# The broadcast gate rows of a hybrid mLSTM / DeltaNet block, issued from GpSimd's DMA queue instead of SyncE's

## The chip, the cores and the metric

The kernel runs on one core of a Trainium2 chip. A core has five engines that run side by side, each with its own instruction stream executed in order: TensorE (PE in the profile; its weight loads are PEld), VectorE (DVE), ScalarE (ACT), GpSimd (POOL) and SyncE (SP), which here does nothing but issue transfers. Transfers are carried by 16 DMA engines; SP, ACT and POOL can each issue them, and each has a queue of its own (q1 is SP's, q10 is ACT's, q0 is POOL's in the profile's table). An engine that issues a transfer waits, in its own stream, until the transfer's target may be overwritten, and the engine that uses the data waits for a semaphore that the landed transfer raises. The metric is device time in microseconds (us) of one launch; lower is better.

## The reference

One decoder layer on 512 tokens of width 2048, all in float32: an RMSNorm, one wide projection, two causal token mixers (8 mLSTM heads and 16 gated DeltaNet heads), an output projection per branch, a gated sum and a final RMSNorm. What matters here is where one number per token and head enters a token-by-token matrix:

```python
# mLSTM: one running gate sum b and one running maximum per head and token
dmat = bcum[..., :, None] - bcum[..., None, :] + ic[..., None, :]
m_t = jnp.maximum(inter_log, dmax_c)
inter_w = jnp.exp(inter_log - m_t)
intra_w = jnp.exp(dm_c - m_t[..., None]) * sc_c
# DeltaNet: one decay sum gam per head and token
rel = gam[..., :, None] - gam[..., None, :]
decay_mat = jnp.where(incl, jnp.exp(jnp.where(incl, rel, 0.0)), 0.0)
q_dec = qc * jnp.exp(gam)[..., None]
```

In each of these the number belongs to the query token `t`. The kernel keeps the query tokens along the free axis of a tile, so that number has to be present in every one of the 128 partitions.

## The kernel before, in words

Matrix products are done in pairs of float32r parts: each weight chunk is loaded (`wr`), rounded to a high part on ACT (`wh`, line 135) and its remainder is formed on DVE (`wl`, line 138), and TensorE multiplies three products per pair. Four chunks may be loaded ahead and four may be split ahead (`NRAW`, `NSPL`).

The stages follow each other: the RMSNorm and the first query and key projections; four kinds of wide projections with a seven-product scheme (to about 1060 us of the span); the mixers with the remaining projections (about 1060 to 1900 us); the output projections and the final norm.

In the gate stage near the start, the per-head rows are computed once with the heads in partitions and stored to a small DRAM tensor `rows_d` of 32 rows by 512 tokens: rows 0 to 7 hold the mLSTM exponents, 8 to 15 the mLSTM inter-chunk weights, 16 to 31 the DeltaNet decay sums (lines 459, 469, 470).

The mixers run as eight DeltaNet units of two heads each (`dn_unit`), `p` = 0 to 7. A unit projects keys, values and queries of its two heads (and, for `p` = 3 to 6, also queries and keys of one mLSTM head, 4 to 7); the mLSTM heads 0 to 3 were projected early and run beside the first units (`ml_first`). Around these projections, small generators (`dn_front_k`, `dn_front_q`, `dn_back`, `dn_chain`, `ml_head`) put out the mixers' own instructions; `tick()` advances them, and `yield n` lets n groups of matmuls go by. The order on TensorE is the order of the program text. On the other four engines a planner that simulates the program's time line orders the instructions: by readiness, by priority (`urgent` raises it) and by the fixed neighbours given with `behind`. Each engine then runs its list strictly in order.

The steps that use the gate rows:

- DeltaNet: `dn_front_k` asks for the rows of its two heads with `row_bcast` (line 760; tile `gb`). GpSimd makes from each a masked copy `dm` (line 823); ScalarE exponentiates `dm` (line 832) and then `gb` in place (line 833); GpSimd copies the last column of each chunk (`ge`, line 834) and much later multiplies the queries with `gb` (line 920).
- mLSTM: `ml_head` asks for one row with `row_bcast` (tile `nrb`) and for one with line 1090 (tile `iwb`). GpSimd makes the masked copy `wm` from `nrb` (line 1093), ScalarE exponentiates it (line 1098); GpSimd takes the last columns of `iwb` (`de`, line 1109) and multiplies the queries with it (line 1111).

`gb` and `nrb` share three buffers (tag `rb`); the last reader of a `gb` is line 920 and the only reader of an `nrb` is line 1093, both on GpSimd. `iwb` shares three buffers (tag `tg`) with the transposed queries `qn` and, in other stages, with other tiles. Every load copies one row of 512 float32 (2 KB) into each of 128 partitions: 256 KB.

Besides these, GpSimd has in a unit the small power functions of the norms (lines 873, 1036, 1157), products with broadcast columns (lines 872, 896, 1037, 1160) and copies of the inverted blocks (lines 937, 940). It issues transfers only after the mixers: the accumulating stores of the output (`y_d`, lines 1339 and 1440).

Of the kernel before, what the change touches and what calls it, by code (L numbers as in the profile page):

```python
# [15 lines left out]
P = 128  # L16
# [39 lines left out]
def hybrid_body(  # L56
# [16 lines left out]
    nc = tc.nc  # L73
    ctx.enter_context(tc.manual_schedule(engines={mybir.EngineType.PE}))
    V, A, G, T = nc.vector, nc.scalar, nc.gpsimd, nc.tensor
# [5 lines left out]
    rows_d = dr.tile([32, S], F32, tag="rows", name="rows_d")  # L81
# [666 lines left out]
    for i in range(NYP):  # L748
        t = wkb.tile([P, S + 3], F32, tag=f"yp{i}", name=f"yp{i}", bufs=1)
# [7 lines left out]

    def row_bcast(r, name):
        t = wk.tile([P, NC, P], F32, tag="rb", name=name, bufs=3)
        nc.sync.dma_start(t.rearrange("p c t -> p (c t)"), rows_d[r, :].partition_broadcast(P))  # L760
        return t

    def bc(col, n):
# [53 lines left out]

    def dn_front_k(hs, kq, u):
        rbs = [row_bcast(16 + h, "gb") for h in hs]
        yield 4  # L820
        for j in range(2):
# [221 lines left out]
    def dn_unit(p, mh):  # L1043
# [13 lines left out]
        if mh is not None:  # L1057
            ps = proj_cm(mh, kind="m")
            mkq = wkb.tile([P, 2, S], F32, tag="mkq", name="mkq", bufs=1)
            with urgent():  # L1060
                A.mul(mkq[:, 1, :], ps[0], float(P) ** -0.5)
            with urgent():
                A.copy(mkq[:, 0, :], ps[1])
            start(ml_head(mh, mkq), 1, "B")
# [18 lines left out]
    def ml_head(h, kq):  # L1083
        kT, qT = kq[:, 0, :], kq[:, 1, :]
        kw = wkb.tile([P, NC, P], F32, tag="mkw", name="kw", bufs=1)
        with behind("V"):
            turn(kT, kw)
        rb = row_bcast(h, "nrb")
        iwb = wp.tile([P, NC, P], F32, tag="tg", name="iwb", bufs=3)
        nc.sync.dma_start(iwb.rearrange("p c t -> p (c t)"), rows_d[8 + h, :].partition_broadcast(P))  # L1090
        yield 4
        w = wkb.tile([P, NC, P], F32, tag="mw", name="wm", bufs=1)
        G.affine_select(out=w, in_=rb, pattern=[[0, NC], [1, P]], channel_multiplier=-1, base=0,
# [74 lines left out]
    def ml_first(h):  # L1168

        kq = wkb.tile([P, 2, S], F32, tag="mkq", name="mkq", bufs=1)  # L1170
        for i in range(2):
            nc.sync.dma_start(kq[:, 1 - i, :], qk_d[2 * QKFIRST * i + h])
        yield 4
        yield from ml_head(h, kq)
# [481 lines left out]
```

## Time and profile before

| | us |
|---|---|
| median of 3 runs | 2229.91 (2222.15 to 2234.51) |
| the profiled execution, its own time | 2228.3 |
| its span, first to last instruction | 2226.5 |
| PE busy | 2157.8 (97% of the span) |
| DVE busy | 1650.0 (74%) |
| ACT busy | 1022.2 (46%) |
| POOL busy | 265.2 (12%) |

The span is what the trace covers; the time of a run is a little longer. Busy time is the sum of an engine's instructions. Where an engine is idle, the profile names the instruction or transfer that ended the idle time. In a row of the time line stand the start, the duration, the engine, the source line, the operation, the target and the source, how many instructions are merged, and in brackets the idle time before with its releaser; a "q" behind the engine marks its sequencer, which issues transfers. A row of transfers "us to landing" counts from the issue until the semaphore is raised.

### The profile page before, as it was taken

How to read it: one execution, taken by the hardware profiler on the slowest of the kernel's cores; microseconds unless marked ns; L12 is line 12 of the kernel's file. 1: busy time of each engine (PE TensorE's matmuls, PEld its weight loads, DVE VectorE, ACT ScalarE, POOL GpSimd, SP SyncE). 2: the span in 40 equal slices, each digit the busy share in tenths (PEclk: the TensorE clock that was granted, in tenths of full speed). 3: DMA queues.
4: the chain of work that ended last, by engine and by line, in shares of the span. 5: the costliest groups of instructions: out<-in, count | busy, mean ns of one | idle time of the engine just before them, and what ended most of it. 6: DMA issues, size and time to landing. Idle time of an engine off the chain costs nothing. (4 is left out here: it accounts for less than half of the span.)

```text
span 2226.5 us, 31649 instructions
## 1 busy us (share of the span) xinstructions
PE 2157.8 (97%) x10592; PEld 1770.6 (80%) x10592; DVE 1650.0 (74%) x2883; ACT 1022.2 (46%) x1986; POOL 265.2 (12%) x356
## 2 busy tenths in 40 slices
PE   6999999999999999999999999999999999989997
PEld 5877878888788788888888788888787887867775
DVE  5787788788778777877597786757575777567776
ACT  5444444445444444444545544444444454334344
POOL 0320000000000000000222412212122211110101
PEclk9999999999999999999999999999999999999999
DMA  5456666667667766776776767767666668695896
GB/s 156 124 176 197 196 202 198 209 200 234 192 211 232 236 197 215 231 241 190 198 201 165 172 161 174 165 160 172 161 145 162 152 157 230 176 268 184 247 323 220
DMA packets 534821, 435.81 MB, mean 196 GB/s; under 512 B 241921, under 2 KB 393698, under 8 KB 534530
## 3 DMA queue, kind: packets, MB, share of 16 engines
q1 hardware_dynamic: 425058, 357.68, 56.3%
q10 hardware_dynamic: 105568, 68.77, 9.7%
q0 software_dynamic: 4032, 7.34, 2.2%
q8 instruction: 83, 1.36, 0.2%
q14 instruction: 80, 0.66, 0.1%
HBM read 342.37 MB, written 95.49 MB: 197 GB/s over the span
## 5 line engine op out<-in xcount | busy, mean ns | idle before, releaser
L135 ACT CAST wh<-wr 128x512 fp32r<-128x512 f32 (+1 forms) x538 | 379.2, 706 | 416.3 <-PE pj L262 229.3
L138 DVE TENSOR_TENSOR wl<-wr,wh 128x512 fp32r<-128x512 f32 (+1 forms) x538 | 440.9, 822 | 152.9 <-ACT wh L135 142.7
L261 PE MATMUL pj<-uh,wh 128*128 128x512 f32 x1024 | 428.6, 419 | 0.0
L263 PE MATMUL pj<-uh,wl 128*128 128x512 f32 x1024 | 402.6, 393 | 0.0
L262 PE MATMUL pj<-ul,wh 128*128 128x512 f32 x1024 | 402.1, 393 | 0.0
L576 PE MATMUL ps<-wl,uh 128*128 128x512 f32 x704 | 277.7, 394 | 6.7 <-DVE wl L138 6.5
L575 PE MATMUL ps<-wh,uh 128*128 128x512 f32 x704 | 276.1, 392 | 6.3 <-DVE X L617 6.0
L577 PE MATMUL ps<-wh,ul 128*128 128x512 f32 x704 | 274.9, 391 | 0.0
L135 ACT CAST wh<-ts 128x512 fp32r<-128x512 f32 x224 | 138.2, 617 | 258.2 <-DVE ts L535 199.7
L135 ACT CAST wh<-t 128x1024 fp32r<-128x1024 f32 x112 | 117.8, 1052 | 250.0 <-PE ps L577 129.2
L263 PEld LDWEIGHTS pj<-uh,wl 128*128 128x128 f32 x1024 | 193.4, 189 | 42.6
L576 PE MATMUL ps<-wl,suh 128*128 128x512 f32 x576 | 224.3, 389 | 1.7 <-DVE wl L138 1.7
L575 PE MATMUL ps<-wh,suh 128*128 128x512 f32 x576 | 224.4, 390 | 0.6 <-ACT wh L135 0.3
L577 PE MATMUL ps<-wh,sul 128*128 128x512 f32 x576 | 224.1, 389 | 0.0
L261 PEld LDWEIGHTS pj<-uh,wh 128*128 128x128 f32 x1024 | 194.3, 190 | 35.2
L262 PEld LDWEIGHTS pj<-ul,wh 128*128 128x128 f32 x1024 | 194.3, 190 | 32.9
L138 DVE TENSOR_TENSOR wl<-ts,wh 128x512 fp32r<-128x512 f32 x224 | 153.7, 690 | 38.5 <-ACT wh L135 38.5
L138 DVE TENSOR_TENSOR wl<-t,wh 128x1024 fp32r<-128x1024 f32 x112 | 137.7, 1229 | 47.5 <-ACT wh L135 46.6
L576 PEld LDWEIGHTS ps<-wl,uh 128*128 128x128 f32 x704 | 132.3, 188 | 43.6 <-DVE wl L138 17.3
L575 PEld LDWEIGHTS ps<-wh,uh 128*128 128x128 f32 x704 | 132.3, 188 | 40.1 <-DVE X L617 12.4
L577 PEld LDWEIGHTS ps<-wh,ul 128*128 128x128 f32 x704 | 132.5, 188 | 26.6
L535 DVE TENSOR_TENSOR ts<-wr 128x512 f32<-128x512 f32 x112 | 77.3, 690 | 102.8 <-DMA wr<-t_d 77.0
(302 smaller groups left out, 3475.6 us busy)
## 6 DMA issues: line engine op xcount, KB each, us to landing
wr<-in_w_in_dram SPq DMA_DIRECT2D x704, 256.0 KB, 3.7
wr<-in_w_out_dram SPq DMA_DIRECT2D x138, 256.0 KB, 5.1
t_d<-ts ACTq DMA_DIRECT2D x96, 256.0 KB, 4.0
wr<-t_d SPq DMA_DIRECT2D x96, 256.0 KB, 4.0
wr<-in_w_in_dram SPq DMA_DIRECT2D x64, 128.0 KB, 3.4
xt<-in_x_dram SPq DMA_DIRECT2D x8, 512.0 KB, 7.3
tg_d<-X ACTq DMA_DIRECT2D x16, 256.0 KB, 6.1
tg_d<-to ACTq DMA_DIRECT2D x16, 256.0 KB, 5.7
```

Of the source, the lines that this page charges most:

```text
L135: newest["A"] = A.copy(hi, src).ins
L138: newest["V"] = V.tensor_tensor(out=lo, in0=src, in1=hi.bitcast(F32), op=ALU.subtract).ins
L261: T.matmul(ps[j], hi[:, k, wsl], uh[:, kt, :], start=(kt == 0), stop=False)
L262: T.matmul(ps[j], hi[:, k, wsl], ul[:, kt, :], start=False, stop=False)
L263: T.matmul(ps[j], lo[:, k, wsl], uh[:, kt, :], start=False, stop=(kt == KT - 1))
L535: V.tensor_tensor(out=ts[:, 0, :], in0=r[:, 0, :], in1=r[:, 2, :], op=ALU.subtract)
L575: T.matmul(ps[t], ah, hi, start=(g == "A" and i == 0), stop=False, skip_group_check=True)
L576: T.matmul(ps[t], ah, lo, start=False, stop=False, skip_group_check=True)
L577: T.matmul(ps[t], al, hi, start=False, stop=(i == KH - 1), skip_group_check=True)
```

## The change

Two calls name another engine; nothing else is edited. `G` is `nc.gpsimd`. With 16 calls of `row_bcast` for `gb`, 8 for `nrb` and 8 loads of `iwb`, 32 transfers of 256 KB move from SP's queue to GpSimd's, and they enter GpSimd's in-order list beside its computing instructions.

```diff
     def row_bcast(r, name):
         t = wk.tile([P, NC, P], F32, tag="rb", name=name, bufs=3)
-        nc.sync.dma_start(t.rearrange("p c t -> p (c t)"), rows_d[r, :].partition_broadcast(P))
+        G.dma_start(t.rearrange("p c t -> p (c t)"), rows_d[r, :].partition_broadcast(P))
         return t
...
         rb = row_bcast(h, "nrb")
         iwb = wp.tile([P, NC, P], F32, tag="tg", name="iwb", bufs=3)
-        nc.sync.dma_start(iwb.rearrange("p c t -> p (c t)"), rows_d[8 + h, :].partition_broadcast(P))
+        G.dma_start(iwb.rearrange("p c t -> p (c t)"), rows_d[8 + h, :].partition_broadcast(P))
         yield 4
```

## The prediction

> **What bounds the kernel now.** I read the page's busy times first, then the stretches, then what TensorE waits for in the stretch that the change touches.
>
> ```profile
> span 2226.5 us, 31649 instructions
> ...
> PE 2157.8 (97%) x10592; PEld 1770.6 (80%) x10592; DVE 1650.0 (74%) x2883; ACT 1022.2 (46%) x1986; POOL 265.2 (12%) x356
> ```
>
> ```profile
> 1100.00:1900.00 800.00, 786.48 (x4539) 655.39 (x4539) 574.11 (x1435) 386.55 (x1010) 193.53 (x257) 0.99 0.70 169
> 1900.00:2226.50 326.50, 299.24 (x1334) 240.47 (x1332) 230.30 (x338) 135.42 (x229) 27.58 (x32) 0.98 0.78 238
> ```
>
> The columns after the length are the busy times of PE, PEld, DVE, ACT and POOL. In the mixers TensorE is idle for only 800.00 − 786.48 = 13.5 us. That is all that any change of a queue can win there; POOL in the same stretch is idle for 800.00 − 193.53 = 606 us. The last stretch has another 326.5 − 299.2 = 27.3 us, but none of the moved loads lies in it. What TensorE waits for in the mixers, from the waits between 1061 and 1910 us (us in total, times, longest):
>
> ```profile
> PE p L974 <- ACT s L970: 4.3, 3, 1.9
> PE pw L1006 <- DVE tb L976: 4.2, 3, 1.9
> ```
>
> These two, 8.5 us together, are its largest waits there. Neither names a gate row. So the question is whether the moved loads, now late only for GpSimd, get late enough for ACT, DVE and at last TensorE.
>
> **What the moved loads cost on SP now.** The two source lines, then who waits for their data, with the landing times (first line 760, then 1090):
>
> ```profile
> L760 SPq DMA_DIRECT2D gb<-rows_d x16: 332/360/552, 1075.3 to 1780.9; - x16
> L760 SPq DMA_DIRECT2D nrb<-rows_d x8: 339/487/1367, 1072.1 to 1674.8; - x8
> DMA to landing us min/median/max: 3.7/4.4/6.0
> L1090 SPq DMA_DIRECT2D iwb<-rows_d x8: 338/465/1082, 1061.0 to 1666.0; - x8
> DMA to landing us min/median/max: 3.6/4.6/4.7
> ```
>
> ```profile
> POOL de L1109 <- DMA iwb<-rows_d: 20.2, 5, 6.4
> POOL dm L823 <- DMA gb<-rows_d: 15.8, 8, 3.7
> POOL wm L1093 <- DMA nrb<-rows_d: 12.0, 5, 3.6
> ```
>
> SP gets rid of 16 × 0.360 + 8 × 0.487 + 8 × 0.465 = 13.4 us of issuing, spread over 700 us. TensorE's two waits above are not for a weight chunk, so this is worth 0 on its path. Only POOL waits for the rows' data, 48 us in all, of its 606 idle.
>
> **What POOL gets.** No load without accumulation is issued from POOL in this trace, so its cost is bounded by the nearest rows, the accumulating stores of line 1339, and by SP's loads of the same bytes:
>
> ```profile
> L1339 POOL DMA_DIRECT2D y_d<-tgy x8: 860/1006/1470, 1893.9 to 1962.3; - x8
> DMA to landing us min/median/max: 4.4/6.9/9.1
> ```
>
> Issue: between SP's 0.36 and 1.47 us; I take the median 1.01, the same engine and form. 32 × 1.01 = 32 us, so POOL's busy time goes from 265 to about 297 us, beside 606 idle: 0 on the path by itself. Landing: 4.4 (as on SP) to 9.1 us. These stores also read and add, a load does not, so the load should be nearer to the store's median from below; I take 6.9, which is 2.5 us later than now. A gate row would then be 1.0 + 2.5 = 3.5 us late. Is there cover? One steady unit, on POOL and SP:
>
> ```profile
> 1666.02 0.47 SPq L1090 DMA_DIRECT2D iwb<-rows_d  x1
> 1670.88 0.33 POOL L1109 COPY de<-iwb 128x4 f32<-128x4 f32 x1 [6.40 <-DMA iwb<-rows_d]
> 1671.17 1.27 POOL L920 TENSOR_TENSOR kq<-kq,gb 128x512 f32<-128x512 f32 x1
> 1672.47 0.34 SPq L760 DMA_DIRECT2D gb<-rows_d  x1
> 1677.05 0.63 POOL L823 TENSOR_SCALAR_AFFINE_SELECT dm<-gb 128x512 f32<-128x512 f32 x1 [2.71 <-DMA gb<-rows_d]
> 1680.37 0.64 POOL L1093 TENSOR_SCALAR_AFFINE_SELECT wm<-nrb 128x512 f32<-128x512 f32 x1 [2.68 <-DMA nrb<-rows_d]
> 1696.92 0.19 POOL L834 COPY ge<-gb 128x4 f32<-128x4 f32 x1 [15.92 <-ACT gb L833]
> ```
>
> The load of `gb` leaves SP at 1672.47, 0.03 us after line 920 has ended (1671.17 + 1.27 = 1672.44): what frees the buffer is POOL's own instruction. Put into POOL's list behind it, this load adds no new wait, only its issue. Three loads (`iwb`, `gb`, `nrb`) follow in a row here; chained on POOL they make its list late by up to 3 × 1.0 + 2 × 2.5 = 8 us at `wm` (the `iwb` wait and one shared wait for the rows). Behind `wm` POOL has nothing until `ge`, after 15.92 us of idling for ACT. So 8 of 15.9 us are used, and the price is 0. If that cover were gone, `ge` and then DVE's line 847 would be late by the rest.
>
> The other reader is ACT's exponent of `dm`. Its smallest distance over the eight units is in the second one:
>
> ```profile
> 1158.10 0.63 POOL L823 TENSOR_SCALAR_AFFINE_SELECT dm<-gb 128x512 f32<-128x512 f32 x1 [2.65 <-DVE tmp L889]
> 1172.39 1.26 ACT L832 ACTIVATE dm<-dm,ngam 128x128 f32<-128x128 f32 x4
> ```
>
> 1172.39 − 1158.73 = 13.7 us, against 3.5 to 8: covered too. One place has no distance, the first mLSTM head:
>
> ```profile
> 1072.32 0.96 POOL L753 MEMSET tb<- 128x1024 f32 x1 [41.67 <-DMA wr<-in_w_in_dram]
> 1075.31 0.64 POOL L1093 TENSOR_SCALAR_AFFINE_SELECT wm<-nrb 128x512 f32<-128x512 f32 x1 [0.84 <-DMA nrb<-rows_d]
> 1076.33 1.28 ACT L1098 ACTIVATE wm<-wm,acol 128x128 f32<-128x128 f32 x4
> ```
>
> ACT takes `wm` 0.38 us after it is there. With the load 3.5 us later (up to 6 if it also queues behind the 0.96 us memset and its neighbours), ACT stands still that long, and weight splits queue behind it. Their cover is the stock of split chunks:
>
> ```profile
> ACT wh L135 <- PE pj L262: 202.8, 135, 4.0
> ```
>
> ACT waits 135 times for TensorE to give a split buffer back, that is, all four are usually full; one chunk here is 12 matmuls, about 12 × 0.39 = 4.7 us by the page's 393 ns rows (L262, L263), so three chunks ahead are some 14 us. Price 0; the 41.67 us of idling also hide the issue of the first two `iwb` loads.
>
> ```profile
> L262 PE MATMUL pj<-ul,wh 128*128 128x512 f32 x1024 | 402.1, 393 | 0.0
> ```
>
> **A possible gain, and a loss.** TensorE's wait for `s` (line 970) has a cause that the moved loads lie beside:
>
> ```profile
> 1673.73 3.53 ACTq L806 DMA_DIRECT2D hm_d<-to  x2
> 1682.27 0.59 ACT L970 ACTIVATE s<-p 64x512 f32<-64x512 f32 x1 [4.21 <-DMA hm_d<-to]
> ```
>
> ACT needs 3.53 us to issue two stores, while SP issues its own loads, the `nrb` among them. If issuing from two engines at once is what slows them, taking 0.49 us out of those 3.53 gives back a seventh of the 8.5 us: −1.2 us; bounds 0 and −8.5. [...]
>
> The loss is where POOL's list leads to DVE:
>
> ```profile
> 1234.96 1.01 POOL L1036 TENSOR_TENSOR rsd<-ssq,mhalf 128x4 f32<-128x4 f32 x1 [18.49 <-DVE ssq L1034]
> 1240.15 0.19 POOL L1109 COPY de<-iwb 128x4 f32<-128x4 f32 x1 [4.18 <-DMA iwb<-rows_d]
> 1241.37 0.69 DVE L1040 TENSOR_TENSOR gz<-po,gz 128x512 f32<-128x512 f32 x1 [3.85 <-POOL gz L1037]
> ```
>
> Here `de` stands in front of the product `gz`, POOL waits 4.18 us for `iwb`, and DVE with it 3.85 us, without any wait of TensorE in the list above for it. The moved load makes this 3.5 us longer; the stock of chunks should cover 7.4 us of 14. I put in +2 us, with bounds 0 and 5 × 3.5 = 17.5 us (every one of the five `iwb` waits passed on whole).
>
> **The sum**, against the profiled execution's own 2228.3 us: 0 (SP) + 0 (POOL's 32 us) − 1.2 + 2 = 2229.1. The median of the runs is 1.6 us above that execution, so 2230.7: 2231 us.
>
> **Rivals.**
> 1. *ACT's queue is relieved fully*: TensorE's 8.5 us go. For it: 3.53 us for two issues is long, and SP is issuing then. Against it: only one of several SP loads leaves that window. 2229.9 − 8.5 = 2221 us.
> 2. *POOL's order passes the lateness on* (the other side): `iwb`'s load and its landing stand in POOL's list ahead of `gz` and the copies for the inverted blocks; DVE stops in order at line 1040. Price 17.5 us, 2247 us. It decides from the point where the wait, 3.85 now, passes the stock of about 14 us, or where TensorE's next small product needs DVE at once. Against it: today's 3.85 us cost TensorE nothing.
> 3. *DVE starves POOL's issuing*: the longest row is 1.47 us to issue and 9.1 to land. If all five `iwb` loads are as late, 5 × (1.47 + 9.1 − 4.6) = 30 us, 2260 us. Against it: the median row is 1.01, in a stretch where DVE is as busy (230.30 of 326.5 us, 71%) as in the mixers (574.11 of 800, 72%). [...]
> 4. *The planner redraws the other lists*: with the loads gone from SP and new entries on POOL, its simulated time line shifts, and near ties on ACT and DVE can fall the other way, in the mixers or behind them. Nothing in the profile says which way; at most the 13.5 us of idle time come back (2216 us), and as much may be lost (2243 us). This is also the way in which the change might not do what it says: a load that the planner puts far down POOL's list comes late whatever its queue costs.
>
> **How the numbers follow.** Half a percent is 11.1 us, about what a measurement of this kernel can tell from no change: 2218.8 to 2241.1. Chances: forecast 0.60 (0.02 of it beyond the lower bound by the scatter of runs, which spans 12 us, 0.03 beyond the upper); rival 1 0.14 (0.05 beyond); rival 2 0.13 (0.11 slower); rival 3 0.03 (slower); rival 4 0.10 (0.06 faster, 0.04 slower). Faster 0.02 + 0.05 + 0.06 = 0.13; slower 0.03 + 0.11 + 0.03 + 0.04 = 0.21; within 0.66. The range 2217 to 2247 us takes in rivals 1 and 2 and leaves out rival 3 and the far side of rival 4.
>
> **What the changed profile would show.** POOL's busy time near 297 us with 32 issues of about 1.0 us on lines 760 and 1090; q0's bytes up by the 32 loads and q1's down; landing of `gb` and `iwb` at 5 to 7 us; POOL's waits for the rows at 60 to 130 us instead of 48 (48 + 32 × 2.5 = 128); PE's idle time between 1100 and 1900 us within some 5 us of 13.5. It would be wrong if DVE's wait at line 1040, or the one of ACT for `wm`, turns up before an idle TensorE (rival 2), if the issues take over 1.5 us (rival 3), if the 3.53 us on ACT's queue shrink together with the waits at lines 974 and 1006 (rival 1), or if TensorE's idle time moves in places without a gate row (rival 4).

## The result, and the profile after

The changed kernel takes 2216.52 us (median, 2214.27 to 2221.79) beside 2229.91 us of the kernel before; the ratio is 0.995 with a 95% interval of 0.9937 to 0.9963. Measured once more beside the last experiments it took 2222.13 us against 2230.99: 0.9961, 0.9949 to 0.9973. So it is faster by some 0.4 to 0.5%. The prediction said 2231 us, range 2217 to 2247. The first measurement lies 0.5 us under that range and just beyond half a percent, the side that had got a chance of 0.13; the second lies inside the range and, by its ratio, within half a percent, which had got 0.66. Both are faster by more than their intervals leave open, where no gain had been forecast.

The profiled execution has an own time of 2217.53 us. Its page begins:

```profile
span 2215.8 us, 31667 instructions
...
PE 2156.6 (97%) x10592; PEld 1770.1 (80%) x10592; DVE 1655.4 (75%) x2883; ACT 1022.3 (46%) x1986; POOL 279.5 (13%) x388
...
q1 hardware_dynamic: 420450, 349.29, 55.3%
q10 hardware_dynamic: 105568, 68.77, 9.8%
q0 software_dynamic: 6592, 15.73, 3.7%
```

All 32 loads are on q0 (the columns are packets, MB and the share of 16 engines). POOL's busy time is up by 279.5 − 265.2 = 14.3 us, where 32 were expected. The issue and landing rows of the two moved lines (first line 760, then line 1090) say why, and POOL's waits for the rows, from 1061 to 1910 us, went down and not up:

```profile
L760 POOL DMA_DIRECT2D gb<-rows_d x16: 536/565/620, 1075.1 to 1769.0; - x16
L760 POOL DMA_DIRECT2D nrb<-rows_d x8: 536/559/571, 1074.4 to 1661.6; - x8
...
DMA to landing us min/median/max: 3.7/4.3/7.7
...
L1090 POOL DMA_DIRECT2D iwb<-rows_d x8: 557/615/775, 1062.1 to 1653.1; - x8
...
DMA to landing us min/median/max: 4.1/4.8/7.8
```

```profile
POOL wm L1093 <- DMA nrb<-rows_d: 12.6, 4, 4.0
...
POOL dm L823 <- DMA gb<-rows_d: 6.1, 6, 2.7
```

An issue costs 0.56 to 0.62 us where 1.01 was taken (16 × 0.565 + 8 × 0.559 + 8 × 0.615 = 18.4 us), and the rows land after 4.3 and 4.8 us, practically as from SP (4.4 and 4.6), where 6.9 was taken. A wait of POOL for `iwb` is not in the list any more.

The time was won in the mixers. The same two stretches, and TensorE's waits between 1061 and 1910 us, all of them:

```profile
1100.00:1900.00 800.00, 793.56 (x4609) 662.07 (x4608) 586.68 (x1450) 391.21 (x1017) 205.20 (x283) 1.00 0.71 173
1900.00:2215.80 315.80, 291.48 (x1268) 234.96 (x1266) 222.74 (x325) 131.51 (x222) 27.27 (x32) 0.97 0.78 238
```

```profile
PE pw L1006 <- DVE tb L976: 4.0, 4, 1.9
PE py L1315 <- ACT yp L770: 2.1, 2, 1.8
PE p L974 <- ACT s L970: 0.3, 1, 0.3
```

TensorE's idle time there is 6.4 us instead of 13.5, and the wait of line 974 went from 4.3 to 0.3 us. TensorE runs the same 10592 matmuls in the same order in both kernels, so the start of each can be compared with the start of the same one before. Up to matmul 4500 (1052 us) the two are 0.6 us apart; at matmul 8750 (1807 us before) the changed kernel is 11.9 us ahead; at matmul 10500, near the end, 8.8 us. So 12.5 us were won in the mixers and some of it was given back after them. Of the 12.5, the idle time explains 7.1. The rest is the granted clock: a window laid on two places of the kernel before (PEclk is the third column from the end) shows 0.50 right behind TensorE's stalls; a matmul of 128x512 takes 0.63 us there where it takes 0.39 before and after, and its next one starts 0.43 us later instead of 0.23.

```profile
1456.80:1460.20 3.40, 3.40 (x19) 2.90 (x18) 2.40 (x4) 2.65 (x5) 0.00 (x0) 0.50 1.01 230
1460.20:1463.60 3.40, 3.40 (x10) 2.63 (x10) 3.37 (x7) 2.14 (x9) 0.00 (x0) 0.50 0.47 101
1576.30:1579.70 3.40, 3.40 (x11) 2.72 (x10) 3.40 (x6) 2.61 (x12) 0.00 (x0) 0.50 0.29 77
```

Three stretches of 3.4 us, 10.2 us in all, at a clock of 0.50 are an estimated 5.1 us lost, and they count as busy (PE 3.40 of 3.40 us in each row). The first follows a stop of 1.91 us of TensorE at line 974 that began at 1454.5, the last a stop of 1.39 us at line 974 (1568.2) and one of 1.91 us at line 1006 (1573.7). The changed kernel's profiled execution has none up to matmul 8750. 7.1 + 5.1 = 12.2 of 12.5 us. What was given back after that goes with the clock, too: up to matmul 10500 the changed kernel has three slow stretches (the first below, behind a stop of 1.77 us at line 1315; then 3.4 us at 1945.6 and 6.8 at 1986.6), the kernel before has one (3.4 us at 1999.5). TensorE is busy for 11.65 us of the three and 3.4 us of the one, so the clock of 0.50 costs the changed kernel by the same estimate some 4 us more there, and 3.1 us were given back.

```profile
1839.80:1843.20 3.40, 3.40 (x9) 2.63 (x10) 3.40 (x9) 2.85 (x6) 0.00 (x0) 0.50 1.20 311
```

### The profile page after: what moved, and what is told of

Same layout as the page of the kernel before. It is cut to its first block, busy times and chain, and to the rows that moved or that the text cites. A ratio compares the mean times of both kernels' runs of the same rounds, so it can differ in the third digit from the quotient of the medians.

```text
span 2215.8 us, 31667 instructions
## 1 busy us (share of the span) xinstructions
PE 2156.6 (97%) x10592; PEld 1770.1 (80%) x10592; DVE 1655.4 (75%) x2883; ACT 1022.3 (46%) x1986; POOL 279.5 (13%) x388
## 4 chain that ended last, share of the span: by engine, by line
PE 71%; DMA 12%; DVE 9%; issue 4%; ACT 2%; SPq 2%; POOL 1%; ACTq 0%; DVEq 0%; POOLq 0%
PE ps L576 10%; PE ps L577 10%; PE ps L575 10%; PE pj L261 9%; PE pj L263 9%; PE pj L262 9%; DVE wl L138 4%; DMA wr<-t_d 4%; DMA wr<-in_w_in_dram 2%; PE py L1315 2%; PE py L1316 2%; PE py L1317 2%; ACT wh L135 1%; SPq L505 1%; DVE X L617 1%
## 5 line engine op out<-in xcount | busy, mean ns | idle before, releaser
L135 ACT CAST wh<-t 128x1024 fp32r<-128x1024 f32 x112 | 117.8, 1052 | 248.6 <-PE ps L577 133.1
```

What stands on the lines that cost most here:

```text
L135: newest["A"] = A.copy(hi, src).ins
```

## What holds ScalarE

The stops at line 974 come from ScalarE's `s` (line 970), and that from ScalarE's stores at line 806. The rows of that line say who waited for these stores, before and after:

```profile
L806 ACTq DMA_DIRECT2D hm_d<-to x64: 309/310/517, 1132.1 to 1796.2; - x64
L806 ACTq DMA_DIRECT2D h_d<-to x64: 309/358/2046, 1244.5 to 1962.1; - x64
...
  ACT wh L135: 15.5, 4
  ACT s L970: 14.0, 3
```

```profile
L806 ACTq DMA_DIRECT2D hm_d<-to x64: 309/310/1210, 1132.5 to 1784.3; - x64
L806 ACTq DMA_DIRECT2D h_d<-to x64: 309/443/2421, 1242.8 to 1951.8; - x64
...
  ACT wh L135: 8.2, 3
  ACT tb L963: 6.3, 2
```

A store of `hm_d` takes 0.31 us to issue, never over 0.52 before. The "3.53 us for two stores" of the prediction is a row in which the time line merged two issues and the wait between them. What lies between can be read from the semaphore that each transfer raises, which the trace numbers. In this program all transfers of SP and ACT raise one of the same eight (100 to 105, 107, 108), given out in turn over both engines (250 or 251 transfers on each in the kernel before); POOL's raise eight others (111 to 118). An issue on a number waits, in its engine's stream, until the previous transfer on that number has landed, whichever engine issued it: for the three held stores below the trace gives that semaphore as what the issue waits for, and on the five numbers of which the trace of the kernel before has every landing, none of 1248 issues starts earlier than 0.016 us behind the previous landing. The kernel before, in the unit that the prediction quoted (worked out from the trace: issue, engine, line, target, semaphore, landing):

```
1672.47 SP  L760 gb    108  lands 1676.93
1674.76 SP  L760 nrb   103  lands 1680.31
1675.41 SP  L1115 v    104  lands 1681.78
1676.95 ACT L806 hm_d  108  (0.02 us after gb)
1680.33 ACT L806 hm_d  103  (0.02 us after nrb)
1681.80 ACT L806 hm_d  104  (0.02 us after v)
```

Three stores in a row were held by three loads of SP, two of them gate rows. ScalarE stood still, `s` started at 1682.27, and TensorE's line 974 at 1682.91. The second wait of TensorE has the same origin. The next rows are DVE and PE of the kernel before, right behind:

```profile
1684.26 0.75 DVE L773 SCALAR_TENSOR_TENSOR kq<-yp,convc,kq 128x512 f32<-128x512 f32 x1 [5.48 <-ACT kq L771]
...
1688.17 0.68 DVE L976 COPY tb<-p 64x512 f32<-64x512 f32 x1
...
1688.91 0.49 PE L1006 MATMUL pw<-vt,tb 128*128 128x128 f32 x2 [1.90 <-DVE tb L976]
```

VectorE had stood 5.48 us waiting for a ScalarE that was held, had to do its queued work first, and came late with `tb`: both waits of TensorE hang on held stores.

Counted over the mixers (1061 to 1910 us; issues that start within 0.15 us of the landing of the previous transfer on their semaphore, and the time that they stood for it), ScalarE was stopped 44 times for 45.8 us before and 29 times for 22.2 us after. Of the 45.8, 9.9 us are `hm_d` behind `nrb`, 9.3 behind `gb`, 5.0 behind `iwb`, and 1.5 are `h_d` behind `nrb`: 25.7 us behind moved loads.

A third stop of TensorE, 1.75 us at line 1128, has two parents. PE and DVE of the kernel before, then PE of the changed one:

```profile
1258.53 0.70 PE L1128 MATMUL pnum<-c,mkq 128*128 128x257 f32 x2 [1.75 <-DVE c L1138]
```

```profile
1252.54 0.75 DVE L773 SCALAR_TENSOR_TENSOR kq<-yp,convc,kq 128x512 f32<-128x512 f32 x1 [4.04 <-ACT kq L771]
...
1258.01 0.47 DVE L1138 SCALAR_TENSOR_TENSOR c<-c,de,pcs 128x257 f32<-128x257 f32 x1
```

```profile
1256.68 0.59 PE L1128 MATMUL pnum<-c,mkq 128*128 128x257 f32 x2
```

DVE needs ScalarE's `kq` first, waits 4.04 us and then 1.40 us for it, and `c` stands behind in its list. Between 1244 and 1256 us ScalarE's stores, here of `h_d`, are held seven times for 7.4 us in the kernel before, and twice for 1.1 us in the changed one. The other parent is the place where the prediction looked for a loss, POOL's product `gz` behind the copy `de`. POOL of the changed kernel there:

```profile
1236.03 1.05 POOL L1037 TENSOR_TENSOR gz<-gz,rsd 128x512 f32<-128x512 f32 x1
1237.03 0.18 POOL L1109 COPY de<-iwb 128x4 f32<-128x4 f32 x1
```

With the loads in POOL's list, the planner puts `de` behind `gz`, and DVE's stop of 3.85 us, shortly ahead of the rows above, is gone. Taking away either parent is enough, as the runs below show: the stores alone on POOL leave `de` ahead of `gz` and have no stop at line 1128; the change measured again has 5.5 us of holds there, its `de` behind `gz`, and no stop; 32 other loads moved, with 5.3 us of holds and `de` ahead of `gz`, keep it.

This is the theory: **the shared semaphores** hold ScalarE's stores behind long loads, and the change wins because 32 of these leave the set. The rivals: **SyncE's issuing time** (13.4 us) or the lateness of its other loads was what counted; or the **planner's other order** won the time.

## The experiments

One table first. "Mixers" is the shift of the profiled execution against the kernel before, between matmuls 4500 and 8750 (about 1052 to 1807 us; negative is faster); "974" is TensorE's waiting at line 974 and "held" are ScalarE's stops as counted above, both from one profiled execution. Times are medians; each ratio is against the kernel before, measured beside it.

| kernel | us | ratio, 95% interval | mixers, us | 974, us | held: times, us |
|---|---|---|---|---|---|
| before | 2229.91 | 1 | 0 | 4.3 | 44, 45.8 |
| the change | 2216.52 | 0.995 (0.9937 to 0.9963) | −12.5 | 0.3 | 29, 22.2 |
| e15 the change again | 2222.13 | 0.9961 (0.9949 to 0.9973) | −7.7 | 0 | 37, 32.4 |
| e1 `iwb` only | 2228.44 | 0.9992 (0.9982 to 1.0002) | −2.8 | 4.2 | 40, 40.4 |
| e2 `gb`, `nrb` only | 2224.01 | 0.9966 (0.9953 to 0.9979) | −4.8 | 1.0 | 46, 41.8 |
| e5 32 other loads instead | 2227.82 | 0.9985 (0.9971 to 0.9998) | −2.2 | 0.6 | 32, 32.6 |
| e6 rows on ACT's queue | 2226.34 | 0.998 (0.9966 to 0.9994) | −3.6 | 0.2 | 43, 38.3 |
| e14 stores alone on POOL | 2214.46 | 0.9925 (0.9913 to 0.9938) | −13.2 | 0 | 1, 0.3 |
| e8 rows and stores on POOL | 2215.28 | 0.994 (0.9918 to 0.9962) | −12.8 | 0 | 0, 0 |
| e3 large copies on SP | 2238.31 | 1.0035 (1.0022 to 1.0049) | +8.2 | 7.9 | 42, 60.8 |
| e16 the same, stores on POOL | 2223.16 | 0.9967 (0.9955 to 0.9979) | −7.8 | 0 | 0, 0 |
| e4 small copies on SP | 2224.80 | 0.997 (0.9956 to 0.9985) | −5.2 | 1.5 | 42, 38.8 |
| e12 small copies on POOL | 2221.27 | 0.9964 (0.9953 to 0.9976) | −8.7 | 0.9 | 30, 29.5 |
| e13 three small copies on SP | 2225.81 | 0.9983 (0.997 to 0.9995) | −6.9 | 0.7 | 38, 41.2 |
| e9 large copies on POOL | 2247.66 | 1.0078 (1.0054 to 1.0103) | +15.8 | 9.5 | 43, 55.4 |
| e7 rows and 32 others | 2220.86 | 0.9949 (0.9932 to 0.9967) | −12.0 | 0 | 30, 27.0 |
| e10 rows and `v` | 2220.88 | 0.9958 (0.9943 to 0.9972) | −12.5 | 0 | 37, 26.3 |

### The two parts of the change

Line 1090 alone:

```diff
-        nc.sync.dma_start(iwb.rearrange("p c t -> p (c t)"), rows_d[8 + h, :].partition_broadcast(P))
+        G.dma_start(iwb.rearrange("p c t -> p (c t)"), rows_d[8 + h, :].partition_broadcast(P))
```

> Only the 8 loads of iwb go to GpSimd; the 24 loads of gb and nrb stay on SP. Theory (shared semaphores): transfers of SP and ACT draw their completion semaphores from one set of eight, and an issuer waits until the transfer that last had the semaphore has landed; a load on GpSimd has a semaphore of another set, so each load moved away shortens such waits on ACT and SP. With 8 of 32 moved, 2 to 5 of the 13 us of the change come back: 2225 to 2228 us; the waits of TensorE at lines 974 and 1006 partly stay. Rival (GpSimd's order): the gain comes from iwb's place in GpSimd's list, because its wait stood in front of the product gz and stopped DVE for 3.85 us; then most of the gain comes with these 8 loads alone: about 2218 us, and TensorE's wait for c (line 1138) is gone.

Line 760 alone:

```diff
-        nc.sync.dma_start(t.rearrange("p c t -> p (c t)"), rows_d[r, :].partition_broadcast(P))
+        G.dma_start(t.rearrange("p c t -> p (c t)"), rows_d[r, :].partition_broadcast(P))
```

> Only the 24 loads of gb and nrb go to GpSimd; iwb stays on SP. Theory (shared semaphores): 8 to 11 of the 13 us come back: 2219 to 2222 us, ACT's wait at line 970 for hm_d stores and TensorE's at lines 974 and 1006 shrink, the stop of DVE at line 1040 for gz stays. Rival (GpSimd's order): 2226 us or more.

`iwb` alone gave 1.4 us (2228.44 against 2229.86, the interval includes no change), `gb` and `nrb` alone 5.9 us. TensorE's waits at line 974 in the one and in the other:

```profile
PE p L974 <- ACT s L970: 4.2, 3, 1.6
```

```profile
PE p L974 <- ACT s L970: 1.0, 1, 1.0
```

The stop at line 1128 is gone with `iwb` alone (matmul by matmul, 1.91 us are won at 1258 us; ScalarE is held there for 1.9 us instead of 7.4, and `de` stands behind `gz`), most of the stops at line 974 with `gb` and `nrb`. The larger part belongs to the 24 loads of line 760. Both gains are a little smaller than the theory had said (2225 to 2228 and 2219 to 2222 us). The second speaks against the planner's other order: with `gb` and `nrb` alone, TensorE, ScalarE and VectorE run all their computing instructions in the same order as before (by line and tile, in order of start); only GpSimd's differ, at two places, and a few of SP's loads change places. In the change itself ScalarE's order is the same, too, and VectorE's differs at two places (lines 1040 and 796). The holds in all do not tell the two kernels apart (40.4 and 41.8 us), so what seems to count is not how long ScalarE is held, but which store is held, those just ahead of `s` and `kq` or others.

### As many other loads

The rows stay on SP; the 16 loads of `gz` (line 1024) and the 16 of `mg` (line 1149), also 256 KB each, go to POOL:

```diff
-                nc.sync.dma_start(g, gz_d[:, :, h * P:(h + 1) * P].rearrange("c p n -> p c n"))
+                G.dma_start(g, gz_d[:, :, h * P:(h + 1) * P].rearrange("c p n -> p c n"))
...
-                    nc.sync.dma_start(g[i], g_d[:, :, col:col + P].rearrange("c p n -> p c n"))
+                    G.dma_start(g[i], g_d[:, :, col:col + P].rearrange("c p n -> p c n"))
```

> The gate rows stay on SP, as before the change; instead 32 other loads of 256 KB of the same stage go to GpSimd: the gate products gz (line 1024, 16) and mg (line 1149, 16). Theory (shared semaphores): which loads are moved matters little, it is the number of transfers that leave the set; 6 to 13 us under before: 2217 to 2224 us, unless one of them makes GpSimd wait in front of gz. Rival (something of the gate rows): no gain, 2228 us or more.

4.1 us won (2227.82 against 2231.93). This missed what the theory had said, that it hardly matters which loads leave the set (2217 to 2224 us). SP is relieved of as many issues of the same size, and the kernel gets less than half of the change's gain. The stop of 1.8 us at line 1128 stays. The number of issues that SP saves is not what sets the gain. (VectorE's list differs from before at 47 places here, so part of the difference may be order.)

### The rows from ScalarE's queue

```diff
-        nc.sync.dma_start(t.rearrange("p c t -> p (c t)"), rows_d[r, :].partition_broadcast(P))
+        nc.scalar.dma_start(t.rearrange("p c t -> p (c t)"), rows_d[r, :].partition_broadcast(P))
...
-        nc.sync.dma_start(iwb.rearrange("p c t -> p (c t)"), rows_d[8 + h, :].partition_broadcast(P))
+        nc.scalar.dma_start(iwb.rearrange("p c t -> p (c t)"), rows_d[8 + h, :].partition_broadcast(P))
```

> All 32 loads are issued from ScalarE's queue. SyncE is relieved of its 13.4 us exactly as in the change, but the loads keep their places among the completion semaphores that SyncE and ScalarE share. Shared set: nothing is won, 2226 to 2245 us, with holds of 40 us or more on ScalarE in the mixers and matmul line 974 waiting for ScalarE's s. SyncE's issuing time: the time of the change, 2214 to 2221 us. A load that stops ScalarE until its tile is free would show as waits of ScalarE at lines 760 and 1090, and would be a reason of its own for a slower kernel.

3.2 us won (2226.34 against 2229.51; the interval of the ratio, 0.9966 to 0.9994, leaves 1.3 to 7.6 us). SP loses the whole of its 13.4 us as in the change, and the semaphores are shared as before. ScalarE is held 43 times for 38.3 us, and SP more than before (29 stops, 40.6 us against 17 stops, 13.2 us). SP's stops alone do not set the time: by the same count they grow with the change as well, to 21 stops and 23.3 us, and it is faster. The time came as the shared set says, one sign did not: line 974 hardly waits (0.2 us), and it is line 1006 that does:

```profile
PE pw L1006 <- DVE tb L976: 6.4, 6, 1.9
```

The lists of DVE and ACT were drawn differently here, too, so the 3.2 us are an upper hint, not a price, of what SP's relief is worth.

### The stores themselves leave the set

The sharpest test leaves the rows where they were and takes the held transfers away. Only the 128 stores of line 806 move, on the kernel before; `behind("A")`, which fixed their place in ScalarE's list, goes with them:

```diff
-                with behind("A"):
-                    nc.scalar.dma_start(d[:, :, a, :].rearrange("m r c -> r m c"), ov[a * BS:(a + 1) * BS])
+                if True:
+                    G.dma_start(d[:, :, a, :].rearrange("m r c -> r m c"), ov[a * BS:(a + 1) * BS])
```

> The kernel before, rows on SyncE's queue as they were, and only the 128 stores of line 806 (hm_d, h_d) are issued from GpSimd's queue. SyncE keeps its 13.4 us of issuing and GpSimd still waits for the rows, but no store can be held behind a row any more. Shared set: the gain of the change comes without the change, 2213 to 2222 us, with hardly any wait of matmul line 974 for s. SyncE's issuing or the rows' landing as the cause: 2226 to 2240 us. GpSimd's list, with 128 issues more (about 70 us), may cost some us of its own at matmul line 1006.

16.5 us won (2214.46 against 2230.99), without the change, and more than by it: measured beside it, the change took 2222.13, and the two intervals of the ratio, 0.9913 to 0.9938 and 0.9949 to 0.9973, do not meet. SP still issues the rows, and POOL still waits for them (31.3 us for `gb`, where it was 15.8). The stretch of the mixers, TensorE's waits in it, all of them, and the rows of the moved stores:

```profile
1100.00:1900.00 800.00, 794.65 (x4621) 662.63 (x4620) 589.61 (x1447) 391.69 (x1018) 275.31 (x377) 1.00 0.69 174
```

```profile
PE py L1315 <- ACT yp L770: 2.4, 2, 1.7
PE pr L998 <- DVE st L1017: 1.4, 1, 1.4
PE pw L1006 <- DVE tb L976: 1.1, 2, 0.7
```

```profile
L806 POOL DMA_DIRECT2D hm_d<-to x64: 648/654/900, 1128.8 to 1772.3; - x64
L806 POOL DMA_DIRECT2D h_d<-to x64: 648/652/1262, 1241.1 to 1947.2; - x64
```

Line 974 is gone from the list and line 1006 falls from 4.2 to 1.1 us. With ScalarE not held, VectorE gets its input earlier and `tb` comes in time:

```profile
1450.78 0.75 DVE L773 SCALAR_TENSOR_TENSOR kq<-yp,convc,kq 128x512 f32<-128x512 f32 x1 [2.88 <-ACT kq L771]
...
1455.50 0.68 DVE L976 COPY tb<-p 64x512 f32<-64x512 f32 x1
...
1456.24 0.49 PE L1006 MATMUL pw<-vt,tb 128*128 128x128 f32 x2
```

128 issues at 0.65 us are 83 us more for POOL, and they show nowhere on TensorE. The stop at line 1128 is gone, too, though `de` still stands ahead of `gz` and waits 2.1 us for `iwb`. This shows that the stores in ScalarE's stream were behind the waits at 974 and 1006 and one of two causes at 1128, and that neither SP's issuing nor the rows' queue had to change for it. What it does not separate: ScalarE is rid of its holds (45.8 us) and of its own issuing (120 issues in the mixers, 44 us) at once, and the planner drew VectorE's list differently at 135 of its 2883 places and ScalarE's at 18 of 1986. That the change won 9 to 13 of the 16.5 us with ScalarE's issuing not shortened (the same 120 issues, 50 us), the lists nearly the same, and holds cut from 45.8 to 22 to 32 us, speaks for the holds; how the rest divides stays open.

Both together, rows and stores on POOL:

```diff
-                with behind("A"):
-                    nc.scalar.dma_start(d[:, :, a, :].rearrange("m r c -> r m c"), ov[a * BS:(a + 1) * BS])
+                if True:
+                    G.dma_start(d[:, :, a, :].rearrange("m r c -> r m c"), ov[a * BS:(a + 1) * BS])
```

(on the changed kernel)

> The kernel after, with the stores of line 806 (128 of 64 KB, hm_d and h_d) issued from GpSimd's queue instead of ScalarE's: the transfers that were held leave the shared set themselves. Shared set: ScalarE's holds in the mixers go from 22 us to under 5 us and SyncE's fall too, line 974 and line 135 no longer wait behind hm_d, and the time is at or under that of the kernel after: 2205 to 2218 us. Against it stands GpSimd's list, which takes some 128 issues of 0.5 to 0.6 us (about 70 us) and must wait for each tile to: if that decides, 2220 to 2245 us with the vector engine waiting for GpSimd's de, gz or tb.

2215.28, 0.994: no different from the stores alone. Once the stores are out of the set, moving the rows wins nothing that can be measured.

### Loads put back into the set

If taking long loads out of the set wins time, putting others in should lose it. The changed kernel gets, at each of the 32 places, a copy of the same 256 KB within device memory on SP's queue, which nobody reads (`du_d` is a new tensor):

```diff
         G.dma_start(t.rearrange("p c t -> p (c t)"), rows_d[r, :].partition_broadcast(P))
+        with behind("S"):
+            nc.sync.dma_start(du_d[r], rows_d[r, :].partition_broadcast(P))
```

(the same behind line 1090; the lines are written out here)

> The changed kernel with 32 further transfers on SP's queue, one beside each moved load: the same row copied to 128 rows of a scratch tensor in DRAM (256 KB each), which nothing reads. GpSimd's list stays that of the changed kernel. Theory (shared semaphores): SP's set is as full as before the change, for as long a landing: 8 to 13 us of the gain go again, 2224 to 2230 us, and ACT's waits at line 970 or 963 come back. Rival (GpSimd's order): the gain stays, 2214 to 2221 us. Rival (SP's issuing time): the gain goes, as here.

The same with one row of 2 KB, `du_d[r:r + 1, :]` from `rows_d[r:r + 1, :]`:

> As the run with the 256 KB copies, at the same places of SP's list, but each copy moves one row of 2 KB. Theory (shared semaphores): a small copy takes a semaphore too, but lands sooner, so less of the gain goes than with the large copies: 2217 to 2224 us, at least 4 us under that run. Rival (SP's issuing time): issuing costs about the same for a small one, so the time is that of the large copies within 2 us. Rival (GpSimd's order): 2214 to 2221 us for both.

The large copies take the kernel to 2238.31, over the kernel before and over the 2224 to 2230 that were expected, with waits at line 974 and 60.8 us of holds; ScalarE's and VectorE's computing lists are those of the change. The small ones leave it at 2224.80, just over the expected 2224 and in its interval (0.9956 to 0.9985) not told from the change (0.9949 to 0.9973). TensorE's two largest waits with the large copies:

```profile
PE p L974 <- ACT s L970: 7.9, 3, 4.3
PE pw L1006 <- DVE tb L976: 4.4, 4, 1.9
```

A copy of 2 KB lands after 3.6 us in the median, one of 256 KB after 6.4. But of the 60.8 us only 5.4 are stores directly behind a large copy; the rest is behind other transfers, which now stand at other places of the turn and land later. And the large copies also carry 8.4 MB, so they were issued from POOL's queue, too, where they take no place in the set:

```diff
-            nc.sync.dma_start(du_d[r], rows_d[r, :].partition_broadcast(P))
+            G.dma_start(du_d[r], rows_d[r, :].partition_broadcast(P))
```

> The changed kernel with the same 32 further transfers of 256 KB into a scratch tensor as in the run with large copies on SP, but issued from GpSimd, each directly behind the load it copies. Bytes on the DMA engines are those of that run. Theory (shared semaphores): GpSimd's transfers have semaphores of their own, so the set of SP and ACT stays as free as in the changed kernel; GpSimd's list gets 32 x 0.56 = 18 us longer beside its idle time: 2214 to 2223 us. Rival (the bytes: the large copies cost because they occupy the DMA engines): as the large copies on SP, 2232 us or more.

This went against the shared set as I had it: 2247.66, even slower. TensorE's largest wait is again line 974:

```profile
PE p L974 <- ACT s L970: 9.5, 3, 4.0
PE pk L845 <- DVE kq L780: 3.0, 2, 1.5
PE pw L1006 <- DVE r L1001: 3.0, 2, 2.4
```

In the mixers transfers land later beside these copies: SP's after 3.75 us in the mean instead of 3.36 of the changed kernel, ACT's after 4.39 instead of 3.96, POOL's other transfers after 5.51 instead of 5.01. The holds read above ended 0.02 us behind the landing of the transfer ahead, so late landings lengthen the holds without a new place being taken (55.4 us of ScalarE). That this is the whole reason was not shown; bytes and holds are not apart in e3 or e9. The next kernel comes nearer to that: e3, and the stores on POOL.

```diff
 (e3, with)
-                    nc.scalar.dma_start(d[:, :, a, :].rearrange("m r c -> r m c"), ov[a * BS:(a + 1) * BS])
+                    G.dma_start(d[:, :, a, :].rearrange("m r c -> r m c"), ov[a * BS:(a + 1) * BS])
```

> The kernel after with the 32 large copies on SyncE's queue (2238.31 us so far) and with the stores of line 806 on GpSimd's queue. The copies keep their bytes (8.4 MB written, 8.4 MB fetched), but the stores are no longer held behind them. Holds of stores: most of the 22 us that the large copies cost are gone, 2215 to 2225 us. Bytes (every transfer lands later beside the copies): 2230 to 2240 us, with SyncE's loads and the weights late.

2223.16, as the holds would have it. But moving the stores is a gain of its own, so the price of the copies is read against e8, which has rows and stores on POOL and no copies: 2223.16 against 2215.28, 7.9 us, or 6 us by the two ratios, whose intervals just touch. With the stores on ScalarE's queue the same copies cost 16 us (2238.31 against 2222.13), or 22 against the first measurement of the change. TensorE's waits:

```profile
PE pr L998 <- DVE st L1017: 4.2, 1, 4.2
PE pw L1006 <- DVE tb L976: 3.5, 2, 2.9
PE py L1315 <- ACT yp L770: 2.4, 2, 1.6
```

So half or more of the loss of e3 came by way of held stores; the rest, some 6 to 8 us, comes with the copies although no store is held, by their bytes or otherwise. (e8 and e16 share one order of ScalarE's and VectorE's lists, the change and e3 another, so each pair is compared within its own.) That it was the copies' own places was not shown (5.4 of 60.8 us); later landings and shifted places do the same. Why the same bytes cost 9 us more from POOL's queue (e9) stays open; that kernel has waits that e3 lacks or has smaller (lines 845 and 1006 behind DVE's `kq` and `r`).

Two more kernels asked whether places alone count, without bytes. One row of 2 KB behind each load, from POOL's queue, and three rows at each place from SP's:

```diff
+        G.dma_start(du_d[r:r + 1, :], rows_d[r:r + 1, :])
```

> The kernel after, with a copy of one 2 KB row in device memory behind each of the 32 loads, that nobody reads: the bytes and the number of copies of the small copies on SyncE's queue (2224.80 us, 0.9970), but issued from GpSimd's queue. Shared set: these copies take no place among the eight completion semaphores of SyncE and ScalarE, so the holds stay where the kernel after has them (ScalarE some 22 us in the mixers, not 39), matmul line 974 waits little, and the time is that of the kernel after, 2214 to 2221 us. The copies themselves (bytes, or any extra transfer): as with the small copies on SyncE, 2222 to 2228 us. GpSimd's time: 32 issues more at about 0.56 us are 18 us of its list; if that is what sets the end, slower than 2228 us with waits on GpSimd's tiles on the vector engine.

```diff
+        for k_ in range(3):
+            nc.sync.dma_start(du_d[k_ * 32 + r:k_ * 32 + r + 1, :], rows_d[r:r + 1, :])
```

> The kernel after, with three copies of one 2 KB row on SyncE's queue at each of the 32 places (96 copies, 0.19 MB in all). Shared set: 96 places of the rotation more, with almost no bytes; holds on ScalarE go from 39 us with 32 copies to 45 us or more, and the time above that of the kernel before: 2228 to 2245 us. If the set is not the cause and only bytes count: the time of the kernel after, 2214 to 2221 us. If only SyncE's own issuing time counts (96 issues at about 0.4 us, 38 us): slower too, but then matmuls wait for loads that are issued late, and not for results of ScalarE.

The first came out as the change does (2221.27). The second missed: 2225.81, not 2228 or more, though 96 more places were taken; it lies between the change and the kernel before. In the list of holds, a single store stands behind a copy, for 1.1 us: 2 KB land after 2.6 us in the median there, mostly before their place comes round again. So the count of transfers in the set does not set the time by itself. That it is which store stands behind which transfer, and for how long, fits e2, e5 and this run, but no run changes that alone.

### More loads out of the set

On the changed kernel, the 32 loads of e5, or the eight loads of `v` (line 1115, 512 KB each, behind which SP's weight loads were held 10.4 us in the changed kernel), go to POOL as well:

```diff
-        nc.sync.dma_start(v1[:, :, 0:NB], v_d[:, :, h * NB:(h + 1) * NB].rearrange("c p n -> p c n"))
+        G.dma_start(v1[:, :, 0:NB], v_d[:, :, h * NB:(h + 1) * NB].rearrange("c p n -> p c n"))
```

> The changed kernel with the 32 loads of gz and mg moved to GpSimd as well, 64 in all. Theory (shared semaphores): the waits on ACT for a shared semaphore shrink further (22 us in the mixers after the change), but TensorE has only 6.4 us of idle time left in that stage: 2210 to 2216 us. Rival (GpSimd's list gets too full: 64 issues, 36 us, and their landings in order): 2218 us or more.

> The changed kernel with the 8 loads of the mLSTM values (line 1115, 512 KB each) moved to GpSimd as well. After the change SP's weight loads are held 10 us behind these loads' landing, and ACT's stores behind those weight loads. Theory (shared semaphores): 0 to 5 us below the changed kernel, 2211 to 2217 us, and the wait for a semaphore on ACT falls below 22 us. Rival (the waits left no longer reach TensorE): 2216 us within 2 us.

2220.86 and 2220.88 us, 0.9949 and 0.9958: not told from the change, and short of the 2210 to 2216 and 2211 to 2217 that the theory had given. What remains held in the changed kernel are mostly `hm_d` stores behind weight loads (11.7 us, and 15.4 us in the repeated profile), and these were not moved.

### The change again

> The changed kernel itself, beside the others on the same chip: 2213 to 2222 us by every theory; it gives the amount that the two others are measured against.

2222.13, just at the upper end of what was expected. Its profiled execution won 7.7 us in the mixers, not 12.5, with 9.7 us of TensorE's idle time left (800.00 − 790.26) and one stretch of 3.4 us at half clock (a matmul of 128x512 takes 0.63 us there, 0.39 before), behind a stop of 1.87 us at line 1006:

```profile
1100.00:1900.00 800.00, 790.26 (x4573) 658.41 (x4571) 584.01 (x1445) 389.83 (x1015) 207.28 (x283) 1.00 0.71 171
```

The two profiled executions of the change thus differ (2217.53 and 2222.13 us); the two medians, 2216.5 and 2222.1, are what a reader should keep.

## Why the prediction was wrong, step by step

- **SP's 13.4 us worth 0.** Not refuted. e5 and e6 relieve SP as much and win 4.1 and 3.2 us, and in each of them other things change as well; e14 relieves SP of nothing and wins 16.5. What the step left out is that SP's loads cost somebody else something: they hold places that ScalarE's stores need (25.7 of the 45.8 us of holds are behind the moved loads).
- **POOL's 32 us, hidden.** Hidden, yes; the size was too large, since the nearest row was an accumulating store. A plain load of a row issued in 0.56 to 0.62 us and landed after 4.3 and 4.8 us, from SP after 4.4 and 4.6.
- **The rows 3.5 us late.** They aren't: POOL waits 18.7 us for them, less than the 48.0 before, where 60 to 130 were expected. The covers that were worked out were never needed.
- **The possible gain of 1.2 us: here the prediction failed.** The place was right (ScalarE's stores, lines 974 and 1006), and the bound of 8.5 us was near what was won. But of its terms the −1.2 us was the wrong one, by its mechanism and by its size: the 3.53 us were read as issuing that two engines slow down for each other, and a seventh was taken for the one load that leaves. The single issues (0.31 us) and what ended the idle time between them show a wait for SP's transfers to land (`gb`, `nrb` and `v`, each 0.02 us ahead of a store). The measured size is 9 to 13 us, the whole of that bound and more. Against SP's time to issue as the cause stands e6: it takes the same 13.4 us from SP (and puts the issues on ScalarE), leaves the loads in the shared set, and won 3.2 us, where the change won 9 to 13.
- **"13.5 us of idle are all that can be won."** Wrong as a bound. e14 won 13.2 us in the mixers with 5.3 us of idle time left: some 5.1 us of the kernel before were lost to matmuls at a clock of 0.50, which count as busy.
- **The loss of 2 us at `gz`.** There was none: the planner moved `de` behind `gz`, and the wait that was to grow went away. That today's 3.85 us cost TensorE nothing was also wrong. The wait of 1.8 us at line 1128 stands in the same list of waits; it lies 17 us later and was not followed back. It hangs on DVE's lateness, to which both this stop and ScalarE's held stores add.
- **The rivals.** Rival 1, that ScalarE's queue is relieved and TensorE's 8.5 us go, is what happened, by another mechanism than "issuing at once"; that its 2221 us lie between the two measurements is partly luck. It got 0.14, because only one of SP's loads was seen to leave the window; in fact three transfers in a row were held there, two of them behind gate rows. Rival 2 (lateness passed on) and rival 3 (slow issues; no run shows that DVE starves them) did not happen: no issue took over 0.78 us, with DVE busy 586.68 of 800 us. Rival 4, the redrawn lists, happened in one place that mattered (`de` behind `gz`); e2, where ScalarE's and VectorE's orders are the old ones, and e14, where `de` is ahead of `gz` again, show gains of 5.9 and 16.5 us without it.

## What to carry to other kernels

When an engine waits between two of its own transfer issues, look at what landed just before the second one. Here a semaphore shared in turn made short stores of ScalarE wait for SP's long loads (25.7 us in the mixers behind the moved ones), and the cure was to take the short ones out of the set (16.5 us), or long ones ahead of them (9 to 13 us), not to save issues. Which long ones mattered: 32 others won 4.1 us. A merged row is no duration of one instruction; split it before it becomes a term of a sum. And count TensorE's idle time and what its time at reduced clock costs together (here 13.5 and some 5.1 us) before saying what a stage can give back.

## What the runs showed of the hardware that I had not expected

- Stops of TensorE of 1.8 to 1.9 us were followed, in the same profiles, by 3.4 or 6.8 us at a granted clock of 0.50, with matmuls of 128x512 of 0.63 us (the windows at 1456.80, 1460.20, 1576.30 and 1839.80 above). Not every stop of that length was: the stop of 1.90 us at line 1006 that ended at 1688.91 was followed by matmuls of 0.39 us at a granted clock of 1.00.
- A plain load issued from GpSimd landed as fast as from SyncE (4.3 and 4.8 us against 4.4 and 4.6) and took 0.56 to 0.62 us to issue against 0.36 to 0.49; a store of 64 KB took 0.65 against 0.31 us.
- 8.4 MB of copies more cost 6 to 8 us where POOL issued 128 short stores (2223.16 against 2215.28) and 16 to 22 us where ScalarE did (2238.31 against 2222.13 and 2216.52).
